# Tree attention on one core: V arrives as fp32 and is cast by the copies that spread it

## The chip, the core and the metric

The kernel runs on one core of a Trainium2 chip. The metric is device time in microseconds, the median of several executions. The kernel before takes 138.03 us (three runs, 137.82 to 138.18). A profile is of one further execution, in which a hardware profiler records what each engine did: PE (TensorE, matrix products), DVE (VectorE), ACT (ScalarE), POOL (GpSimd) and SP, besides the DMA queues. SBUF is the on-chip memory of 128 partitions, PSUM the memory into which PE writes.

## The reference

For 8 x 12 = 96 heads, each with 512 positions of 64 numbers, attention in which position i sees itself and its ancestors in a binary heap (parent of i: (i - 1) // 2), and nothing else:

```python
mask = np.zeros((seq, seq))
for i in range(seq):
    mask[i, i] = 1
    parent = i
    while parent > 0:
        parent = (parent - 1) // 2
        mask[i, parent] = 1
scores = np.einsum('bhqd,bhkd->bhqk', Q, K) * scale
scores = scores + (1 - mask) * (-1e9)
weights = np.exp(scores - np.max(scores, axis=-1, keepdims=True))
weights = weights / (np.sum(weights, axis=-1, keepdims=True) + 1e-10)
return np.einsum('bhqk,bhkd->bhqd', weights, V).astype(np.float32)
```

Q, K, V and the result are fp32 in device memory, 12.6 MB each.

## The kernel before, in words

**Tiling.** Position 4p + t of a head lies in partition p, slot t. The 96 heads make 48 pairs, numbered i, and 12 groups of eight heads (four pairs), numbered g. Of the 512 x 512 scores of a head, only two sets of key tiles are computed: one that holds the top of the tree and one that holds, for each slot, the nodes near the queries; the mask comes from an extra product with sign codes (`k1code`, `q1code`, `k2code`, `q2code`), which pushes forbidden scores far down before the exponential.

**One pair.** PE transposes K and Q of the pair (`transpose`, L250) into a PSUM tile `kqp`; DVE copies that to SBUF as `kq` (`evac`, L276). PE makes the scores (`scores1`, L287 and L292; `scores2`, L310 and L316), ACT takes their exponential (L298, L321). PE multiplies by V (`values`, L347) into the PSUM tile `ob`, with a 65th column of ones that gives the sum of the weights. DVE takes the reciprocal of the sums (L376) and multiplies (L377) into `of`, an fp32 tile of a group (`norm`). There is one `kqp`, one `ob` and one buffer for each kind of score, so each waits for its reader.

**Loads.** `load` (L184 to L192) takes a tile for the group from a pool and issues one transfer from POOL's queue (the issue is line L189). Source and tile differ in type, fp32 and bf16, so the transfer casts. `load_k`, `load_q` and `load_v` call it; the pools `loads` and `vloads` have four buffers for each of `kst`, `qst` and `vst`. The first pair of Q and K comes apart from this, as fp32 through the queues of SP and ACT, and is cast by DVE (L204) and ACT (L205). `plan` lays out the loads by iteration: 12 before the loop, two at i = 1, none at 2, one at 3, two at 4, then one at each iteration to 31, but none at 25 and 29.

**Spreading V.** The key tiles need V's rows in another order over partitions and slots. `spread_top`, `spread_leaves` and `spread_l7` copy blocks of 32 or 64 partitions of `vst` into `vt`, a bf16 tile with room for the column of ones. All of them go through the helper `copy` (L208 and L209), so in the profile every such copy has line L209. `early_copies` deals them out for iterations 2 to 11 over DVE, ACT and POOL. From iteration 12 to 43, `spread` gives each iteration one `spread_l7` of the next group on DVE (32 partitions x 1024), and on POOL two `spread_top` (32 x 512 each) in the first two iterations of a group, or one `spread_leaves` (64 x 1024) in the other two. From iteration 9 on, the first copy on POOL is made to wait for the iteration's last copy on DVE (`after`).

**Stores.** `store` (L385) issues a transfer of a group's `of` from POOL. The pool `opool` has NG = 12 buffers, one for each group. The first eleven stores are issued one per iteration from i = 33 to 43, the last group in three parts at the end.

**Order.** It is written out by hand (`manual_schedule`): each engine runs its instructions in program order. An iteration emits the scores of pair i, values and norm of pair i - 1, transposes and eviction of pair i + 2 (i + 1 before iteration 9), then `spread(i)`, then `pool(i)`, which issues the load or store. So on POOL a transfer's issue stands behind the iteration's copies, and on DVE the copy of V stands behind reciprocal, product and eviction.

Of the kernel before, what the change touches and what calls it, by code (L numbers as in the profile page):

```python
# [98 lines left out]
def kernel(  # L99
# [8 lines left out]
    B, H, S, D = Q.shape  # L108
    P = nc.NUM_PARTITIONS
# [4 lines left out]
    GB = 8  # L114
    NG = NH // GB
    assert NH % GB == 0

    fp32 = mybir.dt.float32
    bf16 = mybir.dt.bfloat16
# [5 lines left out]
    Vr = V.rearrange("b h (p t) d -> p (b h) (t d)", t=4)  # L125
# [10 lines left out]
    vloads = ctx.enter_context(tc.tile_pool(name="vloads", bufs=4))  # L136
    work = ctx.enter_context(tc.tile_pool(name="work", bufs=4))
    etpool = ctx.enter_context(tc.tile_pool(name="etpool", bufs=3))
    small = ctx.enter_context(tc.tile_pool(name="small", bufs=4))
    opool = ctx.enter_context(tc.tile_pool(name="opool", bufs=NG))  # L140
    psS = ctx.enter_context(tc.tile_pool(name="psS", bufs=1, space=bass.MemoryType.PSUM))
    psT = ctx.enter_context(tc.tile_pool(name="psT", bufs=1, space=bass.MemoryType.PSUM))
    psO = ctx.enter_context(tc.tile_pool(name="psO", bufs=1, space=bass.MemoryType.PSUM))
# [37 lines left out]
    qsts, ksts, vsts = {}, {}, {}  # L181
    qTs, kTs, kqps, obs, ets, ofs = {}, {}, {}, {}, {}, {}

    def load(kept, pool, name, src, h0, n):  # L184

        g = h0 // GB
        if g not in kept:
            kept[g] = pool.tile([P, GB, 4, D], bf16, name=name)
        nc.gpsimd.dma_start(  # L189
            out=kept[g][:, h0 % GB:h0 % GB + n, :, :].rearrange("p h t d -> p h (t d)"),  # L190
            in_=src[:, h0:h0 + n, :],
        )  # L192

    def load_k(h0, n=GB):
        load(ksts, loads, "kst", Kr, h0, n)

    def load_q(h0, n=GB):
        load(qsts, loads, "qst", Qr, h0, n)

    def load_v(h0, n=GB):  # L200
        load(vsts, vloads, "vst", Vr, h0, n)

    def first_pair():
        nc.vector.tensor_copy(out=ksts[0][:, 0:2, :, :], in_=first["k"][:, :, :, :])  # L204
# [239 lines left out]
    def plan():  # L444

        k4 = lambda h: [(load_k, h, 4), (load_q, h, 4)]
        seq = [(load_v, 0, 4), (load_k, 2, 2), (load_q, 2, 2)]
        for h in (4, 8, 12):
            seq += k4(h) + [(load_v, h, 4)]
        seq += [(load_k, 16), (load_q, 16), (load_v, 16)]  # L450
        for h in range(24, NH, GB):
            seq += [(load_v, h), (load_k, h), (load_q, h)]
        counts = {-1: 12, 1: 2, 2: 0, 4: 2, 25: 0, 29: 0}
        at = {}
        for i in range(-1, 32):
            n = counts.get(i, 1 if i > 0 else 0)
            at[i], seq = seq[:n], seq[n:]
        assert not seq
        return at
# [97 lines left out]
```

## Time and profile before

| | us | share of the span | instructions |
|---|---|---|---|
| median of three runs | 138.03 | | |
| the profiled execution | 138.54 | | |
| its span | 136.5 | | 5468 |
| PE busy | 112.8 | 83% | 2410 |
| DVE busy | 103.6 | 76% | 215 |
| ACT busy | 90.1 | 66% | 106 |
| POOL busy | 95.9 | 70% | 133 |
| POOL's copies of V | 49.9 | | 73 |
| DVE's copies of V | 28.9 | | 60 |
| ACT's copies of V | 5.2 | | 7 |
| POOL's issues of loads | 36.1 | | 42 |
| POOL's issues of stores | 12.0 | | 14 |

The span runs from the first to the last instruction that the profile shows; an execution has about 2 us around it. The profile's slices cut the span into 40 parts of 3.4 us and give the busy share of each engine in tenths. Rows of groups name line, engine, operation, what is written and read with its shape, how many there are, then busy time and the mean of one in ns, then the idle time of the engine just before them with what ended it. Timeline rows give start, duration, engine, line, operation and in brackets the idle time ahead. The time from issue to landing of a transfer is that of its last part, queueing counted in. The transfers moved 32.3 MB by bytes written; device memory was read for 38.0 MB and written for 12.6 MB.

### The profile page before, as it was taken

To read this page: it belongs to the slowest core of one execution; us is meant where nothing else is said; L and a number is where in the kernel's file an instruction comes from. 1 tells how busy PE (TensorE), PEld (TensorE's weight loads), DVE (VectorE), ACT (ScalarE), POOL (GpSimd) and SP (SyncE) were. 2 spreads that over 40 slices of the span, in tenths; PEclk is the share of its full clock that TensorE was granted. 3 is DMA by queue.
4 is the path that set the end of the run, shared out by engine and by line. 5 is a ranking of instruction groups with operands and counts; after the bars stand their busy time and mean duration, and the time that the engine had idled before them with its cause. 6 is when DMAs were issued, how large, how long until landed. Compare 5 with 4: busy or idle time off the path is not lost.

```text
span 136.5 us, 5468 instructions
## 1 busy us (share of the span) xinstructions
PE 112.8 (83%) x2410; PEld 79.0 (58%) x2410; DVE 103.6 (76%) x215; ACT 90.1 (66%) x106; POOL 95.9 (70%) x133
## 2 busy tenths in 40 slices
PE   6787899896799999997998899898988889698000
PEld 2235576574566777765766576576766667476000
DVE  2466799979799998999889689887989698755300
ACT  4187697749397786875868587866868586577000
POOL 6974979829478899888887578676797777802400
PEclk9999999999999999999999999999999999999655
DMA  3999999999999999999999999999999999999960
GB/s 101 241 186 195 197 196 199 198 198 198 199 197 198 199 199 197 198 200 196 199 197 199 198 199 202 194 200 196 198 326 395 405 400 403 400 407 393 403 256 19
DMA packets 41082, 32.34 MB, mean 237 GB/s; under 512 B 954, under 2 KB 37946, under 8 KB 41058
## 3 DMA queue, kind: packets, MB, share of 16 engines
q0 software_dynamic: 40320, 31.20, 124.7%
q1 hardware_dynamic: 466, 0.53, 1.2%
q8 instruction: 19, 0.31, 0.8%
q10 hardware_dynamic: 272, 0.26, 0.6%
q14 instruction: 5, 0.04, 0.1%
HBM read 38.01 MB, written 12.58 MB: 371 GB/s over the span
## 4 chain that ended last, share of the span: by engine, by line
PE 52%; DMA 20%; issue 11%; POOL 6%; ACT 3%; DVE 2%; POOLq 1%; ACTq 0%
DMA vst<-in_V_dram 20%; PE ob L347 18%; PE kqp L250 11%; PE s L287 8%; PE s L292 5%; PE s L310 5%; PE s L316 5%; POOL vt L209 3%; POOL out_dram L385 2%; ACT e L321 1%; ACT e L298 1%; ACT vt L209 1%; POOL kst L189 1%; POOLq L552 1%; DVE of L377 1%
## 5 line engine op out<-in xcount | busy, mean ns | idle before, releaser
L298 ACT ACTIVATE e<-s 128x1024 bf16<-128x1024 f32 x48 | 49.2, 1025 | 29.7 <-PE s L292 29.3
L209 POOL COPY vt<-vst 32x512 bf16<-32x512 bf16 (+3 forms) x73 | 49.9, 684 | 24.0 <-DVE vt L209 15.3
L347 PE MATMUL ob<-vt,e 128*128 128x65 bf16 (+1 forms) x940 | 38.4, 197 | 3.1 <-issue 1.2
L321 ACT ACTIVATE e<-s 128x768 bf16<-128x768 f32 x48 | 38.7, 807 | 0.2 <-PE s L316 0.2
L347 PEld LDWEIGHTS <-e 128*128 128x128 bf16 (+1 forms) x960 | 30.9, 102 | 11.3 <-issue 2.5
L276 DVE COPY kq<-kqp 128x1024 bf16<-128x1024 bf16 x48 | 32.8, 683 | 3.9 <-PE kqp L250 3.7
L377 DVE TENSOR_TENSOR of<-ob,rec 128x512 f32<-128x512 f32 x47 | 32.5, 691 | 1.6
L209 DVE COPY vt<-vst 32x1024 bf16<-32x1024 bf16 (+2 forms) x60 | 28.9, 481 | 2.6 <-DMA vst<-in_V_dram 1.0
L250 PE MATMUL kqp<-ptile,qst 128*64 128x128 bf16 x384 | 19.5, 220 | 3.2 <-issue 2.8
L250 PE MATMUL kqp<-ptile,kst 128*64 128x128 bf16 x384 | 19.4, 220 | 2.0 <-issue 1.0
L287 PE MATMUL s<-ctile 40*128 40x512 bf16 x96 | 19.1, 386 | 1.7 <-ACT e L298 1.5
L316 PEld LDWEIGHTS <-kq 64*128 64x128 bf16 x384 | 14.4, 94 | 8.4 <-issue 0.6
L292 PE MATMUL s<-kq 64*128 64x512 bf16 x96 | 18.4, 378 | 0.9 <-DVE kq L276 0.9
L310 PE MATMUL s<-ctile 40*128 40x480 bf16 x96 | 18.0, 363 | 0.7 <-issue 0.5
L376 DVE RECIPROCAL rec<-ob 128x8 f32<-128x8 f32 x47 | 9.7, 206 | 11.2 <-PE ob L347 9.5
L316 PE MATMUL s<-kq 64*128 64x64 bf16 (+1 forms) x384 | 17.7, 208 | 0.5 <-issue 0.5
L385 POOL DMA_DIRECT2D out_dram<-of x14 | 12.0, 856 | 6.9 <-DVE of L377 6.9
L250 PEld LDWEIGHTS <-qst 128*64 128x64 bf16 x384 | 13.6, 110 | 3.0 <-issue 2.2
L250 PEld LDWEIGHTS <-kst 128*64 128x64 bf16 x384 | 12.6, 110 | 3.8 <-issue 1.8
L189 POOL DMA_DIRECT2D vst<-in_V_dram x14 | 12.4, 883 | 1.6 <-POOLq L541 0.8
L189 POOL DMA_DIRECT2D qst<-in_Q_dram x14 | 11.9, 849 | 0.0
L189 POOL DMA_DIRECT2D kst<-in_K_dram x14 | 11.8, 844 | 0.0
(22 smaller groups left out, 34.0 us busy)
## 6 DMA issues: line engine op xcount, KB each, us to landing
out_dram<-of POOLq DMA_DIRECT2D x11, 1024.0 KB, 13.0
kst<-in_K_dram POOLq DMA_DIRECT2D x10, 512.0 KB, 12.5
qst<-in_Q_dram POOLq DMA_DIRECT2D x10, 512.0 KB, 13.4
vst<-in_V_dram POOLq DMA_DIRECT2D x10, 512.0 KB, 13.0
vst<-in_V_dram POOLq DMA_DIRECT2D x4, 256.0 KB, 8.9
kst<-in_K_dram POOLq DMA_DIRECT2D x3, 256.0 KB, 8.2
qst<-in_Q_dram POOLq DMA_DIRECT2D x3, 256.0 KB, 9.0
out_dram<-of POOLq DMA_DIRECT2D x1, 512.0 KB, 9.4
```

What stands on the lines that cost most here:

```text
L189: nc.gpsimd.dma_start(out=kept[g][:, h0 % GB:h0 % GB + n, :, :].rearrange("p h t d -> p h (t d)"), in_=src[:, h0:h0 + n, :],)
L209: return (eng.copy if eng is nc.scalar else eng.tensor_copy)(out=out, in_=in_)
L250: nc.tensor.transpose(out=dst, in_=st[2 * i // GB][:, 2 * i % GB + a, t, :], identity=perm)
L276: nc.vector.tensor_copy(out=kq[:, :, :, :].rearrange("p k (x y) c -> p k x y c", y=2), in_=src)
L287: nc.tensor.matmul(out=sp[:, a, :], lhsT=k1code[64 * a:64 * a + BITS, :], rhs=q1code[64 * a:64 * a + BITS, :], start=True, stop=False,)
L292: nc.tensor.matmul(out=sp[:, a, :], lhsT=keys(i, a, TOP), rhs=qTs[i][64 * a:64 * a + 64, :, :].rearrange("p t c -> p (t c)"), start=False, ...
L298: nc.scalar.activation(out=et[:, :, :, :].rearrange("p a t c -> p (a t c)"), in_=sp[:, :, :].rearrange("p a c -> p (a c)"), func=AF.Exp, s ...
L310: nc.tensor.matmul(out=flat[:, a, 32:512], lhsT=k2code[64 * a:64 * a + BITS, :], rhs=q2code[64 * a:64 * a + BITS, 32:512], start=True, sto ...
L316: nc.tensor.matmul(out=flat[:, a, lo:hi], lhsT=keys(i, a, TILE2[t]), rhs=qTs[i][64 * a:64 * a + 64, :, :].rearrange("p t c -> p (t c)")[:, ...
L321: nc.scalar.activation(out=e2s[i % NE][:, :, :, 32:128].rearrange("p a t c -> p (a t) c"), in_=sp[:, :, :, 32:128].rearrange("p a t c -> p ...
L347: nc.tensor.matmul(out=ob[lo:hi, a, 65 * t:65 * t + 65], lhsT=e[:, a, PLACE[t], lo:hi], rhs=vt[:, 2 * i % GB + a, tile_v, 0:D + 1], **flags,)
L377: nc.vector.tensor_tensor(out=ofs[g][:, 2 * r + a0:2 * r + a1, :, :], in0=o4[:, :, :, 0:D], in1=rec[:, :, :, :].to_broadcast([P, a1 - a0, ...
```

## The change

V is loaded into fp32 tiles, so the transfer no longer casts; the tiles of `vst` are twice as large (8 KB instead of 4 KB in a partition, four buffers). The spreading copies, unchanged in the code, now read fp32 and write bf16 into `vt`. To make room, the pool of the output tiles has eleven buffers instead of twelve, so the twelfth group's `of` takes the place of the first group's. K and Q are loaded as before.

```diff
-    opool = ctx.enter_context(tc.tile_pool(name="opool", bufs=NG))
+    opool = ctx.enter_context(tc.tile_pool(name="opool", bufs=NG - 1))
...
-    def load(kept, pool, name, src, h0, n):
+    def load(kept, pool, name, src, h0, n, dtype=bf16):
 
         g = h0 // GB
         if g not in kept:
-            kept[g] = pool.tile([P, GB, 4, D], bf16, name=name)
+            kept[g] = pool.tile([P, GB, 4, D], dtype, name=name)
...
     def load_v(h0, n=GB):
-        load(vsts, vloads, "vst", Vr, h0, n)
+        load(vsts, vloads, "vst", Vr, h0, n, fp32)
```

## The prediction, made before the changed kernel was run

> **What bounds the kernel now.** I read the page's slices and chain first, then the groups of the line that the change touches, then POOL and DVE side by side over a steady stretch, then the landing of the last stores.
>
> ```profile
> DVE  2466799979799998999889689887989698755300
> DMA  3999999999999999999999999999999999999960
> GB/s 101 241 186 195 197 196 199 198 198 198 199 197 198 199 199 197 198 200 196 199 197 199 198 199 202 194 200 196 198 326 395 405 400 403 400 407 393 403 256 19
> PE 52%; DMA 20%; issue 11%; POOL 6%; ACT 3%; DVE 2%; POOLq 1%; ACTq 0%
> ```
>
> The transfers are busy from start to end, at 198 GB/s while loads run and about 400 in the stores. The count is of bytes written: a load reads four bytes for each two it writes, so 198 is 396 read. The chain is V's landing up to 29.8 us (20%), then PE. So there are two runners: a transfer stream that never rests, and a compute loop over pairs of heads that sets when the last stores are issued. Which one wins at the end is read from the stores. The last (256 KB, issued at 127.93) landed after 7.0 us, the one before it (126.29) after 8.0; the plain 256 KB loads at the start, with hardly anything ahead of them, took 3.4 and 3.8. The end is thus the stream's now, and the last store has 7.0 - 3.8 = 3.2 us of queue ahead of it: compute may be that much later for nothing. The span ends 136.5 - 134.9 = 1.6 us after that landing.
>
> What sets the compute loop shows in a timeline, POOL first, then DVE:
>
> ```profile
> 54.68 0.88 POOL L189 DMA_DIRECT2D kst<-in_K_dram  x1
> 55.84 1.27 POOL L209 COPY vt<-vst 32x512 bf16<-32x512 bf16 x2 [0.28 <-DVE vt L209]
> 57.06 0.88 POOL L189 DMA_DIRECT2D qst<-in_Q_dram  x1
> 58.29 1.03 POOL L209 COPY vt<-vst 64x1024 bf16<-64x1024 bf16 x1 [0.35 <-DVE vt L209]
> 59.27 0.88 POOL L189 DMA_DIRECT2D vst<-in_V_dram  x1
> ...
> 55.00 0.78 DVE L209 COPY vt<-vst 32x1024 bf16<-32x1024 bf16 x1
> 55.81 0.21 DVE L376 RECIPROCAL rec<-ob 128x8 f32<-128x8 f32 x1
> 56.05 0.69 DVE L377 TENSOR_TENSOR of<-ob,rec 128x512 f32<-128x512 f32 x1
> 56.66 0.68 DVE L276 COPY kq<-kqp 128x1024 bf16<-128x1024 bf16 x1
> 57.37 0.79 DVE L209 COPY vt<-vst 32x1024 bf16<-32x1024 bf16 x1
> ```
>
> It is a ring. POOL's copies wait for DVE's copy of the iteration (the hand-made dependency), POOL issues a transfer behind them, and DVE's next copy, which starts while that issue runs, takes 0.78 instead of the 0.41 of an undisturbed one (a copy at 52.52) and ends 0.22 us after the issue ends: 54.68 + 0.88 + 0.22 = 55.78, and 57.06 + 0.88 + 0.22 = 58.16, both as shown; eight more between 41 and 75 us do the same within 0.02. Its period is copies 1.21, issue 0.88, 0.22 and 0.06 to start POOL: **2.37** with two 32x512 copies, **2.14** with one 64x1024 (0.98 for 1.21). PE's own round is 2.11 (values start at 43.86 and 45.98). Over iterations 12 to 43 the DVE copy's end went from 44.89 to 117.42, 31 periods in 72.5. The ring gives 13 x 2.37 + 15 x 2.14 + 3 x 2.11 (iterations 25, 29 and 32 issue nothing) = 69.2; the other 3.3 is stalls of PE listed as "issue", of about 0.65 each.
>
> The Trainium skill (SBUF — State Buffer, "Who interferes with whom") says that a VectorE copy of this kind and a GpSimd instruction take one port pair as a lock, the loser blocked to the end of the other. By it the copy would end 0.41 after the issue and not 0.22, and the sums below would be some 5 us longer; the measured rows decide, and they show the clash with a smaller price.
>
> **The change, part by part.** *DVE's copies read fp32.* No row has this shape, but DVE's cast of the first K pair is an SBUF to SBUF copy from f32 to bf16 (first two rows: groups of the first 10 us by shape; third: of the whole span):
>
> ```profile
> L204 DVE CAST kst<-first_k 128x512 bf16<-128x512 f32 x1 | 0.4, 427 | 1.9 <-DMA first_k<-in_K_dram 1.9
> L209 DVE COPY vt<-vst 32x512 bf16<-32x512 bf16 x1 | 0.3, 282 | 0.0
> L209 DVE COPY vt<-vst 32x1024 bf16<-32x1024 bf16 x40 | 22.2, 554 | 1.7 <-DMA vst<-in_V_dram 0.5
> ```
>
> bf16 copies take 0.282 for 512 elements and 0.414 for 1024 undisturbed: 0.132 for each 512 and 0.15 fixed. The cast takes 0.427 - 0.15 = 0.277 for 512, half the rate. So 1024 from fp32: 0.15 + 0.55 = 0.70, **+0.29 a copy**. Bounds: 0 if the strided fp32 copy ran at the bf16 rate, +0.8 if at one element in 1.04 ns (twice the cast); the cast is the nearest row.
>
> *POOL's copies read fp32.* No row. POOL's bf16 times (392, 617 and 1040 ns at 256, 512 and 1024) are 0.85 ns an element. Below, 0; above, twice that if time goes by bytes read, 0.87 us a period. The nearest row is ACT, also 0.85 ns an element in bf16, which takes 0.62 for 512 from f32 (the first Q pair) and 0.61 from bf16. I take **0**. ACT's seven copies: 0, by the same row.
>
> *V's transfers.* Same 1 MB read, twice the bytes written. Plain traffic in the trace runs at 400 (stores) and 374 to 387 (fp32 loads, 3.2 to 4.2 us) against 396 read by cast loads; 12.6 MB in all: 31.2 to 33.3 us against 31.8, so -0.6 to +1.5 on the stream. I take 0: it lies under compute once that ends later. Issue: a plain store of 8 heads costs POOL 0.89, a cast load 0.88, so V's 14 issues change by nothing.
>
> *Eleven output buffers.* The twelfth group's first product (pair 44, DVE at about 120) now waits for the first store, issued at 94.4 and landed 10.8 us later, at 105.2. Margin 15 us, and both move together; cost 0. Without that cover DVE would stand, with the eviction for the next scores behind it and PE behind that.
>
> **The sum.** In the ring the next DVE copy can start 0.03 + 0.24 + 0.61 + 0.71 = 1.59 after the last one ended, and POOL's issue runs from 1.27 (or 1.04) to 2.15 (1.92). The copy still meets it, so it ends 0.29 later than now: **2.66 and 2.43**, and 2.29 where nothing is issued (DVE alone, 1.59 + 0.70). 13 x 2.66 + 15 x 2.43 + 3 x 2.29 = 77.9, against 72.5: +5.4 if PE's stalls vanish in the slack. PE now has 0.55 or 0.32 of it in each period, mean 0.44, so of a stall of 0.65 a third stays: 1.1. **+6.5.** Before that, all waits for V up to 29.8 stay. Iterations 7 to 11 hold eight such copies, 2.3 in all; POOL's copies, for which PE waits at 34.86, stand behind the four of iterations 7 and 8. I take these, **+1.2** (bounds 0 and 2.3). After iteration 43 DVE copies nothing and those 10.5 us stay. The last store is issued 7.7 later, at 135.6.
>
> What is late with it: every load and store behind POOL's copies. Loads land 9.4 to 16 us after issue by the queue, at 2.65 us for each, against 2.55 for an iteration, so the stream stays fed and what lands does not move. Of the stores, the eleventh is issued at 126.4 instead of 118.7 and finds the queue almost empty (it landed at 132.4). The last three therefore go straight through: 135.6 + 3.8 + 1.6 = **141.0 of span**, against 136.5. The profiled execution took 138.54, 2.04 more than its span and 0.5 more than the median; I add the 4.5 to the median: **142.5 us**. Own range: stalls all hidden and no early cost, 140.2; none hidden and all of the early cost, 145.8.
>
> **The rivals.**
> 1. *The stream hides it* (not slower). Place: the end of the store queue; price: nothing as long as the last issue slips by less than 3.2 us, and one for one from there. It needs DVE's copy and POOL's issue to run side by side; then DVE's round of 2.29 gives 71.0 for the 31 periods, under the 72.5 of now. Against it: the ten copies that end 0.22 after an issue. For it: DVE wins where it comes early (46.35 and 52.52, issues stretched to 1.08 and 1.06). Time 138.0.
> 2. *The stream gets shorter.* If 1 holds and plain V loads run at the stores' 400, the end comes 0.6 earlier: 137.4. It decides only while compute slips by less than the 3.2 us. The Trainium skill (DMA: Bandwidth & Descriptors, "Bandwidth") has a plain load of 16 MB at 425 GB/s; by it V would take an estimated 29.6 us and the end could come 2.2 earlier. No run here shows that rate.
> 3. *POOL pays for bytes.* The ring grows by up to 0.87 more in each of 31 periods, 27 us: near 169. A tenth of that, 145. Against it: POOL's 0.85 ns an element matches ACT's, which does not change with f32.
>
> That V arrives as bf16 after all is excluded, since tile and source are both fp32.
>
> **How the numbers follow.** Forecast 0.72, rival 1 0.12, rival 2 0.07, rival 3 0.09. A change under 0.3% (0.4 us) can't be told from none. Faster: rival 2, with a little of 1, 0.08. Same: most of rival 1, 0.10. Slower: the rest, 0.82. The range takes the forecast's own 140.2 to 145.8, goes down to 137.7 for rival 1 and up to 146.5 for small shares of 3; left out are rival 2 and most of 3, with some of the forecast's tails.
>
> **What will show it.** Right: DVE's 32x1024 copies at 0.8 to 1.05 where they meet an issue and 0.70 alone (mean near 0.9, now 0.554); POOL's copies unchanged at 0.61 and 1.04, waiting longer for DVE; starts of POOL's 64x1024 copies in a pair of leaf iterations 2.43 apart; last store's landing under 5 us, and the transfers below 9 tenths in the last slices before it. Wrong: periods still near 2.34 (then the ring is not what binds), POOL's copies longer (rival 3), or a last landing still near 7 us (rival 1).

## The result, and the profile after

The changed kernel takes **139.82 us** (median of 20 executions, 137.74 to 141.08) against 138.09 for the kernel before (20 executions on the same chip, 137.54 to 138.58). The ratio is 1.007, 95% interval 1.0049 to 1.0091; it leaves out executions more than 1.5% above the fastest of the same kernel, ten of the changed kernel's twenty, and so lies below the ratio of the medians (1.0125). The kernel became slower, by less than forecast (142.5 us), and it scatters over 3.3 us where the kernel before scatters over 1.0. The profiled execution took 139.68 us with a span of 137.8 (before 138.54 and 136.5).

From the page of the changed kernel: its busy line, its slices and its chain.

```profile
PE 116.0 (84%) x2409; PEld 80.0 (58%) x2410; DVE 115.3 (84%) x215; ACT 89.6 (65%) x106; POOL 102.8 (75%) x133
PEclk9999999999757999999999999999999999999965
DMA  3999999999999799999999999999999999999991
GB/s 96 329 190 268 277 277 199 369 340 199 343 212 237 214 194 279 246 181 334 197 330 225 262 293 216 336 202 340 214 254 394 372 398 390 394 391 375 397 375 73
DVE 42%; PE 23%; POOL 14%; issue 11%; DMA 4%; POOLq 1%
```

DVE is busy 11.7 us more than before and now leads the chain, in which it had 2%. The transfers are no longer busy throughout: there is a 7 in slice 14, at 45 to 48 us. The rate now swings, since a plain load of V writes as many bytes as it reads. PEclk has a dip at 36 to 43 us that the profile before did not have.

The groups of the changed line, each shape apart:

```profile
L209 DVE CAST vt<-vst 32x1024 bf16<-32x1024 f32 x40 | 31.4, 784 | 1.2
L209 DVE CAST vt<-vst 32x512 bf16<-32x512 f32 x16 | 8.3, 516 | 0.3
L209 POOL CAST vt<-vst 32x512 bf16<-32x512 f32 x40 | 25.0, 624 | 14.4 <-DVE vt L209 10.4 <-DMA vst<-in_V_dram 2.4
L209 POOL CAST vt<-vst 64x1024 bf16<-64x1024 f32 x18 | 18.6, 1035 | 5.6 <-DVE vt L209 5.1
```

POOL's copies cost what they did (617 and 1040 ns before). DVE's mean goes from 554 to 784 ns and, for the short ones, from 357 to 516.

The ring, in a timeline of the changed kernel, POOL first and then DVE, at a place where it runs as forecast:

```profile
82.24 1.03 POOL L209 CAST vt<-vst 64x1024 bf16<-64x1024 f32 x1 [0.89 <-DVE vt L209]
83.23 0.89 POOL L189 DMA_DIRECT2D kst<-in_K_dram  x1
84.75 1.03 POOL L209 CAST vt<-vst 64x1024 bf16<-64x1024 f32 x1 [0.64 <-DVE vt L209]
85.74 0.88 POOL L189 DMA_DIRECT2D qst<-in_Q_dram  x1
87.17 1.27 POOL L209 CAST vt<-vst 32x512 bf16<-32x512 f32 x2 [0.55 <-DVE vt L209]
...
83.93 0.69 DVE L209 CAST vt<-vst 32x1024 bf16<-32x1024 f32 x1
86.21 0.89 DVE L209 CAST vt<-vst 32x1024 bf16<-32x1024 f32 x1
```

DVE's copy starts while POOL's issue runs and ends 0.50 and 0.48 us after it (0.22 before); the first takes its 0.69 all the same, the second is stretched to 0.89. The periods are 2.51 and 2.42, as worked out (2.43). Thirty microseconds earlier the same timeline shows another order:

```profile
53.15 1.09 POOL L189 DMA_DIRECT2D kst<-in_K_dram  x1
54.28 1.03 POOL L209 CAST vt<-vst 64x1024 bf16<-64x1024 f32 x1
55.26 1.25 POOL L189 DMA_DIRECT2D qst<-in_Q_dram  x1
56.56 1.04 POOL L209 CAST vt<-vst 64x1024 bf16<-64x1024 f32 x1
...
53.00 0.75 DVE L209 CAST vt<-vst 32x1024 bf16<-32x1024 f32 x1
55.34 0.69 DVE L209 CAST vt<-vst 32x1024 bf16<-32x1024 f32 x1
```

Here DVE's copy starts 0.15 us ahead of the issue or 0.08 us behind its start, takes 0.75 and 0.69 (0.68 alone), and it is the issue that is stretched, from 0.88 to 1.09 and 1.25. POOL does not wait for DVE (no brackets), the period is 56.56 - 54.28 = 2.28, and it is DVE's own round. Most of the stretches from 50 to 76 and from 107 to 123 us look like this: of the 32 steady copies 19 keep their time and stretch the issue, and nine are stretched themselves.

Where the 1.3 us of span came from, by POOL's copies and the last store:

| | before | after | difference |
|---|---|---|---|
| POOL's copies of iteration 12 start | 44.96 | 49.33 | +4.37 |
| from there to those of iteration 43 | 72.62 | 74.08 | +1.46 |
| from there to the issue of the last store | 10.35 | 8.78 | -1.57 |
| last store issued | 127.93 | 132.19 | +4.26 |
| last store landed | 134.9 | 136.3 | +1.4 |

So three quarters of the delay arise ahead of iteration 12 and a quarter in the steady ring, and most of a delay of 4.3 us at the last issue is taken up by the queue of stores.

### The profile page after: what moved, and what is told of

Its sections match the earlier page's. It is cut to its first block, busy times and chain, and to the rows that moved or that the text cites. A ratio compares the mean times of both kernels' runs of the same rounds, so it can differ in the third digit from the quotient of the medians.

```text
span 137.8 us, 5468 instructions
## 1 busy us (share of the span) xinstructions
PE 116.0 (84%) x2409; PEld 80.0 (58%) x2410; DVE 115.3 (84%) x215; ACT 89.6 (65%) x106; POOL 102.8 (75%) x133
## 4 chain that ended last, share of the span: by engine, by line
DVE 42%; PE 23%; POOL 14%; issue 11%; DMA 4%; POOLq 1%
DVE vt L209 18%; DVE of L377 12%; DVE kq L276 10%; PE ob L347 9%; POOL vt L209 7%; PE kqp L250 5%; DMA qst<-in_Q_dram 4%; DVE rec L376 3%; PE s L287 3%; POOL vst L189 2%; PE s L292 2%; PE s L310 2%; POOL out_dram L385 2%; PE s L316 2%; POOL kst L189 2%
## 5 line engine op out<-in xcount | busy, mean ns | idle before, releaser
L209 POOL CAST vt<-vst 32x512 bf16<-32x512 f32 (+3 forms) x73 | 50.6, 692 | 23.1 <-DVE vt L209 15.5
L347 PE MATMUL ob<-vt,e 128*128 128x65 bf16 (+1 forms) x940 | 39.6, 199 | 8.2 <-DVE of L377 2.9
L209 DVE CAST vt<-vst 32x1024 bf16<-32x1024 f32 (+2 forms) x60 | 41.0, 683 | 1.8 <-DMA vst<-in_V_dram 0.2
L347 PEld LDWEIGHTS <-e 128*128 128x128 bf16 (+1 forms) x960 | 31.6, 103 | 18.1 <-issue 4.5
L276 DVE COPY kq<-kqp 128x1024 bf16<-128x1024 bf16 x48 | 32.8, 683 | 1.4 <-PE kqp L250 1.1
L377 DVE TENSOR_TENSOR of<-ob,rec 128x512 f32<-128x512 f32 x47 | 32.5, 691 | 1.6
L292 PE MATMUL s<-kq 64*128 64x512 bf16 x96 | 18.9, 389 | 2.8 <-DVE kq L276 2.8
L385 POOL DMA_DIRECT2D out_dram<-of x14 | 14.1, 1010 | 5.4 <-DVE of L377 5.4
L189 POOL DMA_DIRECT2D vst<-in_V_dram x14 | 13.9, 995 | 1.3 <-POOLq L541 0.8
L189 POOL DMA_DIRECT2D qst<-in_Q_dram x14 | 13.2, 941 | 0.0
L189 POOL DMA_DIRECT2D kst<-in_K_dram x14 | 13.0, 931 | 0.0
```

The costliest lines, as they stand in the source:

```text
L189: nc.gpsimd.dma_start(out=kept[g][:, h0 % GB:h0 % GB + n, :, :].rearrange("p h t d -> p h (t d)"), in_=src[:, h0:h0 + n, :],)
L209: return (eng.copy if eng is nc.scalar else eng.tensor_copy)(out=out, in_=in_)
L276: nc.vector.tensor_copy(out=kq[:, :, :, :].rearrange("p k (x y) c -> p k x y c", y=2), in_=src)
L292: nc.tensor.matmul(out=sp[:, a, :], lhsT=keys(i, a, TOP), rhs=qTs[i][64 * a:64 * a + 64, :, :].rearrange("p t c -> p (t c)"), start=False, ...
L347: nc.tensor.matmul(out=ob[lo:hi, a, 65 * t:65 * t + 65], lhsT=e[:, a, PLACE[t], lo:hi], rhs=vt[:, 2 * i % GB + a, tile_v, 0:D + 1], **flags,)
L377: nc.vector.tensor_tensor(out=ofs[g][:, 2 * r + a0:2 * r + a1, :, :], in0=o4[:, :, :, 0:D], in1=rec[:, :, :, :].to_broadcast([P, a1 - a0, ...
```

## The experiments

Ratios are to the kernel before, run on the same chip, with their 95% intervals.

**Parts of the change alone.** The output buffers (e1, on the kernel before) and DVE's copies (e2 to e4, on the changed kernel). In e2, DVE's copies read the fp32 rows as 16-bit integers, half of each row, so that they run at the old rate while V still arrives as fp32; DVE's share of V is then not V. e3 does this in iterations up to 11 alone, e4 from 12 on alone.

```diff
-    opool = ctx.enter_context(tc.tile_pool(name="opool", bufs=NG))
+    opool = ctx.enter_context(tc.tile_pool(name="opool", bufs=NG - 1))
```
```diff
+    def vsrc(eng, g):
+        t = vsts[g][:, :, :, :]
+        if eng is nc.vector and now[0] < 12:   # e2: always; e4: >= 12
+            t = t.bitcast(mybir.dt.uint16)
+        return t
...
-            vsts[g][0:32, h0:h1, UNITS[TOP + j][1], :],
+            vsrc(eng, g)[0:32, h0:h1, UNITS[TOP + j][1], 0:D],
```

> The kernel before with eleven output buffers and nothing else. All theories: no wait appears, since the first store had landed at 105.2 us and the twelfth group's first product comes near 120; time within 0.3% of before (138.0 +- 0.4). If the buffers were the cost, DVE would wait for a store ahead of pair 44 and the time would rise by about the 1.0 us seen.

Measured: 138.01 us, 0.9998 (0.9976 to 1.002). The buffers cost nothing.

> The changed kernel, but DVE's copies read the first half of each fp32 row as 16-bit words, so DVE moves as many elements as before the change at the old rate; its part of V is not V. POOL's and ACT's copies read fp32 as in the change. Theory (DVE's slower copies are the whole loss): DVE 32x1024 copies back to 0.41 alone, last store issued near 128, as before the change, time 137.5 to 138.2. Rival (the plain transfers or POOL's and ACT's copies carry part of the loss): last issue still 1 us or more later than 128 and time above 138.5.

> As e2, but only DVE's copies up to iteration 11 are at the old rate; those from 12 on read fp32. Theory (the early, dense copies cost 4.1 us of compute, the steady part 1.5, and the stream hides 3): iteration 12's DVE copy back near 45 us instead of 49.3, last issue near 128 to 129.5, time 137.8 to 138.5. Rival, the split of the prediction (6.5 in the steady part, 1.2 early): last issue later than 133 would be left, time not under 139.

> As e2, but only DVE's copies from iteration 12 on are at the old rate; the early ones read fp32. Theory: iteration 12's DVE copy still at about 49 us, the steady stretch at 2.30 to 2.35 a period, last issue near 130 to 131.5, time 138.0 to 139.0. Rival, the split of the prediction: early cost 1.2 only, last issue near 129, time as before the change.

Measured: e2 136.65 us, 0.9904 (0.9876 to 0.9931); e3 136.48 us, 0.9874 (0.9852 to 0.9896); e4 138.97 us, 1.0031 (1.0002 to 1.006). The groups of e3, by shape, show the edit:

```profile
L209 DVE CAST vt<-vst 32x1024 bf16<-32x1024 f32 x32 | 24.2, 755 | 1.0
L209 DVE CAST vt<-vst 32x1024 bf16<-32x1024 uint16 x8 | 4.4, 556 | 0.6 <-DMA vst<-in_V_dram 0.5
```

Three things follow. With DVE's copies at their old rate the change is a gain of 1.0% to 1.3%: V's plain transfers make the kernel faster, which I had put at nothing. With the early copies at the old rate the 32 fp32 copies of the steady ring cost nothing that can be seen: from iteration 12 to 43 POOL's copies take 73.16 us in e2 and 73.37 in e3, and e3 is no slower. The loss belongs to the copies up to iteration 11: putting them back turns e3's 0.9874 into 1.007, a loss of 2.0% or 2.7 us (by the medians 3.3, 136.48 to 139.82). e4, with only these slow, has four fifths of that loss by the ratios. The last fifth may be the steady copies after all, though the intervals of e4 and the changed kernel overlap: from iteration 12 to 43 the late e4 takes 71.68 us in its profile and catches up, where the changed kernel takes 74.08.

**Is the end set by the last issue or by the store queue?** Twelve products of zeros (about 2.6 us) ahead of pair 44, whose loads and V copies are all done, in the kernel before (e7) and the changed one (e8).

```diff
     def finish(i):
+        if i == 44:
+            fill(i, 12)
         values(i)
```

> The kernel before with twelve products of zeros ahead of values of pair 44, about 2.6 us of PE time in the tail. If the store queue hides 3.2 us, as the prediction had it: last store issued near 130.5, landing 4 to 5 us after issue, time within 0.6 us of before (138.0 to 138.6). If compute sets the end: 140.6.

> The same twelve products in the changed kernel. The queue has nothing left to hide there (the last landing took 4.1 us): 2.2 to 2.6 us over the changed kernel's 139.8, so 141.5 to 142.4. If the stream still hid it: 139.8 to 140.4.

Measured: e7 138.17 us, 1.0012 (0.9986 to 1.0037); e8 139.93 us, 1.0103 (1.005 to 1.0156). By its median e8 is no slower than the change alone (139.82), and its interval, from four executions, covers the change's 1.007; a delay of 2.2 us or more would show. So the delay is free in both within the noise, which I had expected of the kernel before only. The reason shows in the last transfer: its time from issue to landing (last column) in the views of the transfers around its issue, first before, then changed, then e8.

```profile
out_dram<-of POOLq DMA_DIRECT2D x1, 256.0 KB, 7.0
```
```profile
out_dram<-of POOLq DMA_DIRECT2D x1, 256.0 KB, 4.1
```
```profile
out_dram<-of POOLq DMA_DIRECT2D x1, 256.0 KB, 2.4
```

In e8 the last store lands 1.2 us after the one before it, where queued stores of this size land 0.65 apart, so it no longer stands in a queue: a store of 256 KB alone takes about 2.4 us, not the 3.8 that I had taken from loads at the start. So the kernel before has 7.0 - 2.4 = 4.6 us to spare and the changed one still 4.1 - 2.4 = 1.7; e8's last issue, at 134.04, is 1.85 later than the changed kernel's. In e7's profile the last issue comes at 132.63, 4.7 later than before and not the 2.6 expected, and its store, too, takes 2.5: the slack is just used up, and the span is 136.6 against 136.5. The Trainium skill (DMA: Bandwidth & Descriptors, "Anatomy of one DMA") gives 2.0 us plus the bytes over 436 GB/s, which is an estimated 2.6 for this store; the 2.4 agrees.

If queued stores set the end, the last load's landing should set it, with twelve groups of output behind it at 2.6 us or a little more each. The landings in the profiles (us, good to 0.1), with those of runs told further below:

| kernel | last load landed | last store issued | last store landed | load to store |
|---|---|---|---|---|
| before | 102.6 | 127.9 | 134.9 | 32.3 |
| changed | 103.9 | 132.2 | 136.3 | 32.4 |
| e2 | 101.8 | 129.8 | 134.2 | 32.4 |
| e3 | 101.4 | 131.5 | 134.1 | 32.7 |
| e6 | 101.8 | 130.7 | 134.2 | 32.4 |
| e7 | 102.1 | 132.6 | 135.1 | 33.0 |
| e8 | 103.6 | 134.0 | 136.5 | 32.9 |
| e9 | 102.7 | 131.0 | 135.7 | 33.0 |
| e10 | 101.0 | 127.8 | 133.2 | 32.2 |
| e12 | 107.0 | 135.1 | 139.5 | 32.5 |
| e14 | 101.1 | 131.4 | 133.9 | 32.8 |

The issue of the last store varies against its landing by 4.6 us; the last load does not, within 0.8. In e3, e7, e8 and e14 the last store goes through in 2.4 to 2.6, so there the issue sets the end as much as the queue does. (Two profiles lie outside: e4, its last load at 105.0, with 31.2, and e13 with 34.3, where the first two stores landed 5.0 and 6.8 us after their issue, so that their queue was thin: few transfers stood in it. e3's profiled execution has a span 1.0 us above the middle of its others.) So in the profiles the changed kernel ends later than e3 by what delayed its last load, from 101.4 to 103.9.

**Why the last load comes later.** Half-microsecond windows of the changed kernel around slice 14; the last two columns are the DMA share (1.45 for casting loads, about 1.0 for plain ones) and the rate:

```profile
46.00:46.50 0.50, 0.50 (x24) 0.50 (x24) 0.50 (x1) 0.50 (x2) 0.28 (x1) 1.00 0.51 205
46.50:47.00 0.50, 0.50 (x11) 0.24 (x8) 0.47 (x2) 0.42 (x1) 0.09 (x1) 1.00 0.27 99
47.00:47.50 0.50, 0.50 (x12) 0.34 (x9) 0.47 (x2) 0.19 (x1) 0.50 (x1) 1.00 1.02 100
47.50:48.00 0.50, 0.22 (x10) 0.14 (x5) 0.50 (x2) 0.50 (x1) 0.50 (x2) 1.00 0.47 71
48.00:48.50 0.50, 0.50 (x22) 0.45 (x21) 0.47 (x2) 0.50 (x2) 0.50 (x1) 1.00 1.13 137
```

From 46.5 to 48.5 us the transfers move 71 to 137 GB/s, where casting loads move 198. The load of K that should have been in flight was issued at 45.40, against 41.58 before, because its issue stands behind POOL's copies, which wait for DVE's. POOL's timeline, first before, then changed:

```profile
40.35 1.27 POOL L209 COPY vt<-vst 32x512 bf16<-32x512 bf16 x2 [0.72 <-DVE vt L209]
41.58 0.89 POOL L189 DMA_DIRECT2D kst<-in_K_dram  x1
```
```profile
44.17 1.27 POOL L209 CAST vt<-vst 32x512 bf16<-32x512 f32 x2 [2.33 <-DVE vt L209]
45.40 0.89 POOL L189 DMA_DIRECT2D kst<-in_K_dram  x1
```

Loads issued between 41 and 53 us landed 6.2 to 7.9 us later, where before it was 9.4 to 12.0. Five loads landed 3.3 to 3.6 us after the one ahead of them, where 2.6 is the stream's own pace; e3 has two gaps of 3.0 or more, the kernel before one. Three of the five, landed at 51.5, 57.7 and 61.1, had been issued only 6.2 to 7.9 us before. The others are not of this kind: gaps of 3.3 us and more where the load had been issued some 10 us or longer before stand in other profiles too (before at 70.7, e3 at 64.9).

The first test of this, e9, issues each load ahead of the copies in iterations 5 to 12. e11 is the same order in the kernel before.

```diff
-        spread(i)
-        pool(i)
+        if 5 <= i <= 12:
+            pool(i)
+            spread(i)
+        else:
+            spread(i)
+            pool(i)
```

> The changed kernel, but in iterations 5 to 12 POOL issues its load ahead of its copies of V instead of behind them, so the issue no longer waits for DVE's early copies. Theory (DVE's longer early copies hold POOL, POOL issues the loads of iterations 9 to 11 too late, and the stream runs dry at 46 to 48.5 us; that, and not compute, is what moves the end): no stretch under 150 GB/s between 40 and 60 us, the load stream as in e2 (last load landed near 102 instead of 103.9), time 137.0 to 138.6 against 139.8. Rival (compute alone sets the end, issued 4.3 us late): time stays 139.3 or more.

> The kernel before with e9's order of issues, the control. Its stream never runs dry, so nothing is to gain: 137.6 to 138.4 against 138.0. If the order of issues by itself were worth the gain expected of e9, this too would fall by 1 us or more.

Measured: e9 139.84 us, 1.0151 (1.0108 to 1.0194), no better than the changed kernel; e11 137.99 us, 1.0009 (0.9989 to 1.003). The control does nothing, and the gain expected of e9 did not come. Its windows show that the dry stretch is gone:

```profile
47.00:47.50 0.50, 0.50 (x24) 0.45 (x22) 0.47 (x2) 0.50 (x1) 0.50 (x1) 1.00 1.43 233
47.50:48.00 0.50, 0.50 (x18) 0.38 (x14) 0.50 (x1) 0.06 (x1) 0.11 (x1) 1.00 1.42 193
```

But its loads of the iterations behind 12 were again issued late and landed 6.9 to 8.4 us after issue, and in seven of the eleven microseconds from 57 to 68 the stream moved 154 to 189 GB/s. The thin place had moved. That left two readings: the stream, thin further on, or the late computation by itself.

Next, V's loads of groups 5 to 11 went to SP's queue, where they wait for their buffer alone (e12; `load` takes the queue as one more argument).

```diff
-        load(vsts, vloads, "vst", Vr, h0, n, fp32)
+        load(vsts, vloads, "vst", Vr, h0, n, fp32, nc.sync if h0 >= 5 * GB else nc.gpsimd)
```

> The changed kernel, with V's transfers of groups 5 to 11 issued in SP's queue, where they wait for their buffer alone and for nothing in POOL's program; K, Q, the stores and all copies as in the changed kernel. Theory, that the changed kernel's end is set by its stream of transfers, held up because its issues stand in POOL's program behind late copies: the last load lands before 102.0 us (103.9 in the changed kernel), the last store 32.2 to 33.0 us after it, and the time is 136.0 to 137.3. Rival, that the late early copies delay the computation itself and the stream is not what counts: the last load lands earlier all the same, but the last store's issue stays at 131 us or later and the time stays at 138.7 to 140.0.

Measured: 142.58 us, 1.0313 (1.0285 to 1.034). Both expectations missed. V now runs beside K and Q and not in turn with them, and K's and Q's loads issued from 44 us on land 10 to 17 us after issue. In the groups by shape PE now waits 3.8 us for Q, against 0.4 in the changed kernel:

```profile
L250 PEld LDWEIGHTS <-qst 128*64 128x64 bf16 x384 | 13.9, 112 | 5.2 <-DMA qst<-in_Q_dram 3.8 <-issue 1.4
```

It says nothing for the late computation, though: the last load came at 107.0 and the end 32.5 behind it, as everywhere.

Last, the issues of loads alone: ahead of the copies in all iterations from 5 to 31 (e13, the diff of e9 with 31 for 12), and the whole plan moved up by one iteration, POOL's order kept (e14).

```diff
-        counts = {-1: 12, 1: 2, 2: 0, 4: 2, 25: 0, 29: 0}
+        counts = {-1: 12, 1: 2, 2: 1, 4: 2, 25: 0, 29: 0}
```

> The changed kernel with each load issued ahead of the iteration's copies in POOL's program in all iterations from 5 to 31, not behind them. All work is the same. If the changed kernel's end is set by the stream of transfers, which runs thin because its loads are issued late, every load keeps more than 8.5 us from issue to landing, the last load lands at 102.4 us or before (103.9 in the changed kernel, 102.7 where only iterations 5 to 12 were turned round), and the time is 136.8 to 138.6. If the late computation itself sets the end, the loads land earlier all the same and the time stays at 139.2 to 140.2.

> The changed kernel with the plan of loads moved up by one: one load at iteration 2, which had none, so that each later load is issued one iteration (about 2.3 us) sooner; POOL's order within an iteration is kept, and the copies and their number are the same. If the stream sets the end: no dry stretch between 45 and 61 us, the last load lands before 102.2 us, the time is 136.3 to 138.2. If the late computation sets it: last load earlier, time 139.2 to 140.2.

Measured: e13 138.85 us, 0.9986 (0.9948 to 1.0023); e14 139.34 us, 1.0042 (1.0006 to 1.0079). Both medians lie below the changed kernel's, neither in the range that the stream alone would give, and e14's lies in the range of the late computation. (The ratios of the medians are 1.006 and 1.009.) By spans, whose medians are 136.7 in e13 and 136.5 in e14 against 137.85 in the changed kernel and 136.1 before, both win back about two thirds or more of what the change lost. e13 is no clean test: three of its loads, issued at 42.8 to 48.6, still landed only 7.1 to 7.5 us later. e14's profile shows its landings as expected: 2.5 to 2.7 us apart from 40 to 68 us, the last load at 101.1, the last store at 133.9, a span of 135.4. Its page has no dip of the clock:

```profile
PEclk9999999999999999999999999999999999999995
```

Its twelve executions split by the mean granted clock: the seven at 0.980 or above have spans of 135.3 to 136.5, the five at 0.956 or below 137.3 to 138.7. The 23 executions of the kernel before in that batch have spans of 135.6 to 136.7 at clocks from 0.942 to 0.981, with no such split. So with the loads earlier and a high clock the loss against the kernel before is gone (not that against e3, with spans of 134.2 to 134.6 in five of its six), which supports the stream; in e14 some 2 us more go with a lower clock. Elsewhere the mean clock does not sort the executions so: the changed kernel's three at 0.977 or above have spans of 135.7 to 136.9, but those at 0.963 to 0.969 run from 136.6 to 139.1, and e9's six, five of them at 0.979 or above, from 137.2 to 139.0.

**The clock.** In the changed kernel's windows (third column from the end: granted clock):

```profile
36.00:37.00 1.00, 0.58 (x10) 0.48 (x11) 0.97 (x2) 0.11 (x1) 0.00 (x0) 0.55 1.11 405
39.00:40.00 1.00, 1.00 (x14) 0.58 (x11) 0.68 (x1) 0.70 (x1) 0.25 (x1) 0.50 1.43 200
42.00:43.00 1.00, 1.00 (x6) 0.33 (x6) 0.97 (x3) 0.10 (x1) 0.00 (x0) 0.54 1.49 205
```

From 36.1 to 42.9, for 6.8 us, PE runs at half clock. The profiles of e2, e3, e4, e6 and of e7, which is the kernel before but for a late delay, have such a dip between 33 and 45 us; e11 to e13 have one elsewhere; e1, e5, e8 to e10 and e14 have none before the end. So the kernel before can have it too. The late last load does not need it: e8, which is the changed kernel up to pair 44, has no dip, and its last load still landed at 103.6.

```profile
PEclk9999999999999999999999999999999999999985
```

The dip alone does not make the last load late either: e2, e3 and e7 have it, and theirs landed at 101.8, 101.4 and 102.1, all ahead of the 102.6 of the kernel before. I tried to price it by keeping PE busy: four products of zeros ahead of the first scores of pairs 7 to 10 and the values of pairs 6 to 9.

```diff
+        if 7 <= i <= 10:
+            for k in range(4):
+                nc.tensor.matmul(
+                    out=sp[:, k % 2, :], lhsT=zeros[:, 0:128], rhs=zeros[:, :],
+                    start=True, stop=True,
+                )
...
     def finish(i):
+        if 6 <= i <= 9:
+            fill(i, 4)
```

> The changed kernel with products of zeros added on PE: four ahead of scores1 of pairs 7 to 10 and four ahead of values of pairs 6 to 9, all overwritten. Theory (PE's idle gaps at 33 to 36.4 us, where it waits for DVE's longer early copies, drop its granted clock to 0.50 for some 6.5 us in most executions, and that is part of the loss and of its spread): no slices under 9 between 34 and 45 us, median 138.3 to 139.0 against 139.8 for the change, and a spread under 2 us instead of 3.3. Rival (the clock drop costs nothing that the DVE-bound stretch does not cost anyway): median stays 139.5 to 140.

Measured: 142.48 us, 1.0323 (1.0292 to 1.0353). No dip, but each of the eight sets took 1.04 us on PE and PE could not spare it. The run says nothing of the price of a dip.

**A version that keeps both halves of the finding.** e6 leaves V's first four groups, which the early copies spread, as casting transfers to bf16 (at the old rate for DVE) and loads the other eight as fp32. e10 is e6 with the order of e9.

```diff
+    vwide = ctx.enter_context(tc.tile_pool(name="vwide", bufs=4))
...
-        load(vsts, vloads, "vst", Vr, h0, n, fp32)
+        if h0 < 4 * GB:
+            load(vsts, vloads, "vst", Vr, h0, n)
+        else:
+            load(vsts, vwide, "vwide", Vr, h0, n, fp32)
```

(`vloads` has three buffers and `opool` ten to make room.)

> Groups 0 to 3 of V are loaded as bf16 by a casting transfer, as before the change; groups 4 to 11 as fp32, as in the change (output pool ten buffers, three bf16 and four fp32 buffers for V). Correct result. Theory (the early copies are the loss, the steady copies are free, the plain transfers shorten the stream by about 1.6 us in all, two thirds of it here): 136.6 to 137.3, faster than before and than the change. Rival (the steady copies at half rate cost what the plain transfers gain): 138.0 or more.

> e6 (V of groups 0 to 3 as bf16 by a casting transfer, the others as fp32) with e9's order of issues. Correct result. Theory: the stream has no dry stretch in either, so little is left to gain: 136.2 to 137.0 against e6's 136.9. Rival (issues ahead of the copies delay the copies that PE waits for): 137.3 or more.

Measured: e6 136.91 us, 0.9917 (0.9885 to 0.9948); e10 136.51 us, 0.991 (0.9882 to 0.9938), with executions from 136.38 to 137.15. Both beat the kernel before by some 0.9% and the changed one by more, with the whole computation kept.

## Why the prediction was right or wrong

The direction was right, and 139.8 lies in the range of 137.7 to 146.5, but below the forecast's own 140.2 to 145.8. The sum failed in five of its steps, some against each other.

- **DVE's copy at 0.70** was right: 0.68 to 0.69 alone. The forecast mean near 0.9 was not: 0.784, since 19 of the 32 steady copies kept their time beside an issue.
- **POOL's and ACT's copies at no cost**: right (624 and 1035 ns; ACT's 612 for 512). Rival 3 is out. **Eleven buffers at no cost**: right, by e1.
- **"The copy still meets it, so it ends 0.29 later than now"**, and with it +6.5 for iterations 12 to 43, was the largest error: +1.46 in the profile, nothing between e2 and e3, and 2.4 between e4 and the changed kernel. The period of 2.43 was right for the order that I described, but the ring does not stay in it. Once DVE's copy starts ahead of the issue, or at most 0.18 us behind its start, it keeps its time, the issue takes the stretch behind it, and the ring runs at DVE's 2.28. This is rival 1's mechanism. I had quoted two places where DVE wins, at 46.35 and 52.52, and taken them for exceptions.
- **"All waits for V up to 29.8 stay", and +1.2 ahead of iteration 12**: failed in the other direction, +4.37. A timeline of DVE, first of the kernel before, then of the changed one:

```profile
29.76 1.16 DVE L209 COPY vt<-vst 32x1024 bf16<-32x1024 bf16 x2 [0.53 <-DMA vst<-in_V_dram]
32.52 1.39 DVE L209 COPY vt<-vst 32x1024 bf16<-32x1024 bf16 x2
```
```profile
31.37 1.74 DVE L209 CAST vt<-vst 32x1024 bf16<-32x1024 f32 x2
33.14 0.69 DVE L276 COPY kq<-kqp 128x1024 bf16<-128x1024 bf16 x1
```

  DVE no longer waits for V's landing (no brackets): it comes to this copy 1.6 us later than before. The sixteen shorter copies, 0.16 longer each, make 2.5, and I had left them out as covered by that wait. In e3, where they run at the old rate, the wait is back (0.45 ahead of the copy at 29.31). From 31 to 48 us the delay grows by 2.5 more. Of the 4.1 by which DVE's copy of iteration 12 is late (48.37 against 44.28), most comes of the copies: without the dip of the clock it is 3.7 late in e8 (47.95) and 2.9 in e9 (47.19), whose order differs. That would leave 0.4 to 1.2 for the dip; e2, with the dip and copies at the old rate, starts POOL's copies 1.16 late.
- **V's transfers at 0, bounds -0.6 to +1.5**: the kernel with plain loads and the old copies (e2, e3) is 1.3 to 1.7 us faster, outside my bounds. (By the quoted 400 and 374 GB/s they come to -0.3 and +1.9.) Rival 2 had the mechanism, at too small a size, since I took the stores' 400 for it. By the 425 GB/s of the Trainium skill (DMA: Bandwidth & Descriptors, "Bandwidth") I had an estimate of 2.2, which lies on the other side.
- **"The stream stays fed and what lands does not move"**: failed. I compared the pace of loads and iterations, 2.65 and 2.55, and did not take the delay off the smallest time from issue to landing. That was 9.4 us, as in iteration 10; the issues of iterations 10 to 13 slipped by 3.8 to 4.7, and the time fell to 6.2. The last load came 1.3 us later than before and 2.5 later than in e3.
- **A slack of 7.0 - 3.8 = 3.2 us**: it is 4.6, since a lone store takes 2.4; e7 used it up at no cost. The last issue came 4.26 later, not 7.7, and so the last store still stood in a queue (4.1). "Under 5 us" was right, and "the last three go straight through" was not.

In sum: plain loads give about 1.5 us, and the early copies and what follows from them take most of 2.7 (3.3 by the medians); the steady copies take nothing where the early ones are fast, and 0.5 to 0.9, not clear of the noise, where they are slow. That the early copies are most of the loss is shown by e2, e3 and e4. That it goes by way of thin loads is supported by e7, e8, the landings and e14's profile, but neither e13 nor e14 brought the whole loss back, and e14's median lies where the late computation would put it. The drop of the clock is not needed for the loss (e8) and costs nothing in e7; what it adds in an execution of the changed kernel, and how often that has it, stays open.

## What to carry to other kernels

A cast moved from a transfer to a copy is paid where the copying engine is already behind, so cost it stage by stage: here 28 early copies decided, and 32 later ones, each at least as long, cost little or nothing. Before calling a stream safe, look at the smallest time from issue to landing among its loads and at what the issue stands behind in its engine's program. When two engines collide in a ring, work out the period for either winner; the ring may settle in the cheaper one.

## What the runs showed of the hardware that I had not expected

- The clash of a DVE copy and a transfer's issue on POOL has two outcomes, by when the copy starts. Nineteen copies of the changed kernel that started between 0.18 us ahead of the issue's start and 0.18 us behind it took 0.68 to 0.78, and the issue took 1.08 to 1.35 in place of 0.88. Nine that started 0.30 to 0.48 us behind it took 0.89 to 1.09 and ended 0.49 us behind the issue (0.22 when the copy reads bf16). The Trainium skill (SBUF — State Buffer, "SBUF: two separate sides") says that the one that starts first holds the port pair to its end. The eight copies that started ahead of the issue agree. Eleven that started 0.07 to 0.18 us behind it kept their time all the same, and a copy of 0.69 blocked to the issue's end would end 0.69 behind it, not 0.49; both differ from the page.
- PE's clock fell to 0.50 for 6.8 us, at 36.1, within the second of two gaps of PE of 0.97 and 0.94 us, from 32.9 and 35.5 us. The Trainium skill (TensorE: Matmul & The Clock Gate, "Part 1") names one idle window of about 3.4 us as the cause. No gap here was near that long, and e9, with gaps of 1.19 and 0.94 at the same places, kept its clock.
- V's plain loads in a queue of their own (e12) did not speed the stream: the last load came 3.1 us later than in the changed kernel and the time is 2.8 longer. Whether by the order of K and Q alone was not tried.
